# The convolution taps of the up-projection and the product behind them, each issued one step later

## Chip, core and metric

The kernel runs on one core of a Trainium2 chip. The metric is the device time of one execution in microseconds, as the median of several runs. TensorE (PE) does the matrix products, VectorE (DVE) and ScalarE (ACT) the elementwise work, GpSimd (POOL) and SyncE (SP) issue transfers here.

## What is computed

The reference is one decoder layer on 512 tokens of width 1024: three token mixers, a merge, and a gated MLP with a causal convolution of width 3. The change lies in the MLP's first half:

```
def causal_dwconv3(u, w, b):
    up = jnp.pad(u, ((0, 0), (2, 0), (0, 0)))
    return up[:, :s] * w[0] + up[:, 1:s + 1] * w[1] + up[:, 2:] * w[2] + b
...
    h2 = rmsnorm(x, g_ffn)
    a, b = jnp.split(h2 @ w_up, 2, axis=-1)
    a = causal_dwconv3(a, ffn_conv_w, ffn_conv_b)
    x = x + (jax.nn.silu(a) * b) @ w_down
```

The hidden width is 2816, which is 22 blocks of 128 channels. One block f of a with the same block of b is called a pair here.

## The kernel before

All data are float32. Since TensorE takes rounded operands, each operand is cut in two: a high half (hi, ScalarE, a rounding copy) and a low half (lo, VectorE, source minus hi), and a product is three matmuls (hi with hi, lo with hi, hi with lo). Each low half therefore waits for its high half. Weights come from memory in pieces of 128x1024 (ra, rb, raw), issued by SP.

The up-projection is laid out by hand. A list `steps` holds what TensorE does, one step after the other, and a table `jobs` holds what the other engines do behind each step. `at(i, job)` puts a job behind step i. `later(gen, 0)` runs a generator up to its first `yield` now, and every further part one step later. What lands in the table first is issued first, and VectorE, ScalarE, POOL and SP work in exactly that order in this stretch.

Pairs 6 to 20 are fast pairs: instead of eight half-size products (128x256 outputs over four blocks of depth) they use seven, with sums of weights and sums of inputs. A step is one such product, 12 matmuls. The head of a pair is four steps with the outputs y, z, x, w, the tail three steps that add to z, x, w. The order is head f, tail f-1, head f+1, tail f. Even pairs use the banks s, m, s, m, odd pairs four banks acc; two pairs later the banks are used again. The lines that matter, by engine:

- VectorE: 1199 and 1203 form the sums of weights (sx); 1222, 1223 and 1227 add up the head's outputs; 1244 forms another weight sum; 1250 and 1257 empty z and w behind the tail, 1257 into u, the padded input of the convolution; 998 is the low half of a cut; 1077 the two taps; 1094 (or 1087 for four pairs whose result is stored to memory and read back) the product of the Silu with b.
- ScalarE: 986 is the high half of a cut; 990 a negative of it, to which POOL's accumulating transfer (993) adds the source; 1218 and 1254 copy y and x out; 1074 the first tap with the bias; 1081 the Silu.
- POOL: 1200 adds one weight piece to another by an accumulating transfer (ra gets raw or rb added); the cut of ra waits for it.

In `taps_of` line 1074 is issued behind the tail's last step, the taps one step later, the Silu one more, and the product one more. `taps_of` is called for pairs 0 and 1 by `first_pairs` and for each fast pair by `p3_done`.

Of the kernel before, what the change touches and what calls it, by code (L numbers as in the profile page):

```python
# [123 lines left out]
def layer_kernel(ctx: ExitStack, tc: tile.TileContext, xT, memT, vecs, ws, outT):  # L124
# [22 lines left out]
    def tmp(n=S, dt=F32):  # L147

        i = tmps[0]
        if i is not None:  # L150
            tmps[0] = (i + 1) % 10
            if i >= 8:
                return cm.tile([P, n], dt, tag="tmp", name=nm("tmp"), bufs=2)
        return tp.tile([P, n], dt, tag="tmp", name=nm("tmp"), bufs=8)
# [743 lines left out]
    def taps(f):  # L898
        return [V("f_w", NF * i + f) for i in range(3)], V("f_b", f)
# [170 lines left out]
    def taps_of(f, u, b):  # L1070

        ws, bias = taps(f)
        t = tmp()
        nc.scalar.activation(t, u[:, 0:S], AF.Identity, bias=bias, scale=ws[0])
        yield
        for i in (1, 2):
            nc.vector.scalar_tensor_tensor(
                t, u[:, i : S + i], ws[i], t, op0=ALU.mult, op1=ALU.add
            )
        yield  # L1080
        nc.scalar.activation(t, t, AF.Silu)
        yield
        gate_up(f, b, t)

    def gate_up(f, b, t):
        if f in SPILL:
            nc.vector.tensor_mul(t, b, t)
            nc.sync.dma_start(md[f], t)
            mf[f] = None
            return  # L1090
        n = sum(m is not None for m in mf.values())
        pool, tag = (fm, "mf") if n < NF - 8 - len(SPILL) else (mp, "mj")
        m = pool.tile([P, S], F32, tag=tag, name=nm("mf"))
        nc.vector.tensor_mul(m, b, t)
        mf[f] = m
# [9 lines left out]
    def first_pairs():  # L1105
        for f in range(2):
            u, b = padded(), tmp()
            nc.vector.tensor_mul(u[:, 2 : S + 2], accs[2 * f], r2b)
            nc.vector.tensor_mul(b, accs[2 * f + 1], r2b)
            later(taps_of(f, u, b), 0)  # L1110
# [126 lines left out]
    def fast_tail(f, q):  # L1237
        t = len(steps)
        i2 = 2 * (f - 2) + 3
        n = KH * P  # L1240

        def sums_4():
            sx = q["sx"]
            nc.vector.tensor_sub(sx[:, :n], raws[base + i2][:, :n], sx[:, :n])  # L1244

        w2 = cut_raw(i2, t, t + 1, by_dma=True, lead=LEAD + 3)
        w4 = cut_at(t + 2, t + 2, lambda: q["sx"][:, :n], known=lambda h: at(h - 2, sums_4))

        def p4_done():
            nc.vector.tensor_add(q["b"][:, :H], q["z"][:, :H], q["v"][:, H:])  # L1250
            q["u"] = padded()

        def p2_done():
            nc.scalar.activation(q["u"][:, 2 : H + 2], q["x"][:, :H], AF.Copy)

        def p3_done():
            nc.vector.tensor_add(q["u"][:, H + 2 :], q["w"][:, :H], q["v"][:, H:])
            later(taps_of(f, q["u"], q["b"]), 0)

        steps.extend((  # L1260
            (lambda: product(q["z"], w2, KH, sums[3], False), p4_done),
            (lambda: product(q["x"], w2, 0, rows(KH, 0), False), p2_done),
            (lambda: product(q["w"], w4, 0, rows(KH, H), False), p3_done),
        ))
# [133 lines left out]
```

## Time and profile before

| | |
|---|---|
| median of 3 runs (lowest to highest) | 827.24 us (827.23 to 827.34) |
| profiled execution, and its span | 826.2 us, 824.4 us |
| TensorE busy | 815.3 us, 99% of the span |
| TensorE weight loads | 695.0 us, 84% |
| VectorE busy | 569.7 us, 69% |
| ScalarE busy | 436.3 us, 53% |
| POOL busy | 95.7 us, 12% |
| granted TensorE clock | 1.00 in every stretch (2.4 GHz) |

The span runs from the first to the last instruction of the profiled execution; its time also holds what lies around that. The shares are averages over stages: the fast pairs run from about 534 to 687 us, and in them VectorE is much busier than over the span as a whole.

### The profile page before, as it was taken

The page shows a single profiled execution, that of the slowest core. Times are in us where ns is not written, and L with a number is a line of the kernel's source. Part 1 is how long each engine was busy: PE and PEld are TensorE (multiplying, and loading weights), DVE is VectorE, ACT ScalarE, POOL GpSimd, SP SyncE. Part 2 cuts the span into 40 slices and gives each one's busy share as a digit, 9 for nine tenths or more (in the row PEclk, how much of TensorE's full clock was granted, in tenths as well). Part 3 has the DMA queues.
Part 4 walks back from the last instruction along what each step waited for, and adds up shares of the span by engine and source line. Part 5 has one row for each costly group of instructions (what it writes and reads, how often), then busy time and mean ns, then how long its engine had stood idle before and what let it go on. Part 6 is the DMA issues. An engine that isn't in the chain of part 4 may idle for free.

```text
span 824.4 us, 11450 instructions
## 1 busy us (share of the span) xinstructions
PE 815.3 (99%) x4254; PEld 695.0 (84%) x4254; DVE 569.7 (69%) x963; ACT 436.3 (53%) x779; POOL 95.7 (12%) x134
## 2 busy tenths in 40 slices
PE   9999999999999999999999999999999999999998
PEld 7888788888888888888888888899999998888888
DVE  6998898957767777666466587768888888523221
ACT  7676776736655645554334476556656568312210
POOL 0300000101221011110000022222222220000000
PEclk9999999999999999999999999999999999999999
DMA  8453122333332332225334375677777886433310
GB/s 304 131 179 105 58 96 77 117 120 97 118 100 90 107 97 77 80 100 179 102 99 145 126 197 150 156 182 174 180 179 179 206 191 219 140 102 130 113 64 26
DMA packets 38263, 109.08 MB, mean 132 GB/s; under 512 B 4416, under 2 KB 5056, under 8 KB 38080
## 3 DMA queue, kind: packets, MB, share of 16 engines
q1 hardware_dynamic: 29856, 93.34, 33.9%
q0 software_dynamic: 8208, 14.95, 10.6%
q8 instruction: 33, 0.54, 0.3%
q14 instruction: 22, 0.18, 0.1%
q10 hardware_dynamic: 144, 0.08, 0.0%
HBM read 85.01 MB, written 5.24 MB: 109 GB/s over the span
## 4 chain that ended last, share of the span: by engine, by line
PE 77%; DMA 8%; issue 7%; DVE 3%; POOL 3%; ACT 1%; SPq 0%; POOLq 0%; ACTq 0%; DVEq 0%
PE acc L258 19%; PE acc L259 19%; PE acc L260 19%; DMA ra<-raw 5%; PE s L259 4%; PE s L260 4%; PE s L258 4%; POOL lo L993 2%; DMA ra<-rb 2%; PE m L774 1%; PE m L1184 1%; DMA raw<-ws 1%; PE m L260 1%; PE m L259 1%; PE m L258 1%
## 5 line engine op out<-in xcount | busy, mean ns | idle before, releaser
L223 DVE TENSOR_TENSOR lo<-raw,hi 128x1024 fp32r<-128x1024 f32 (+2 forms) x106 | 128.9, 1216 | 126.4 <-ACT hi L220 125.9
L220 ACT ACTIVATE hi<-raw 128x1024 fp32r<-128x1024 f32 (+2 forms) x106 | 110.3, 1041 | 151.1 <-PE acc L260 85.3
L260 PE MATMUL acc<-h,hi 128*128 128x512 f32 x360 | 142.1, 395 | 0.0
L259 PE MATMUL acc<-h,lo 128*128 128x512 f32 x360 | 142.1, 395 | 0.0
L258 PE MATMUL acc<-h,hi 128*128 128x512 f32 x360 | 142.1, 395 | 0.0
L260 PEld LDWEIGHTS acc<-h,hi 128*128 128x128 f32 x360 | 67.7, 188 | 16.1
L259 PEld LDWEIGHTS acc<-h,lo 128*128 128x128 f32 x360 | 67.7, 188 | 15.3
L258 PEld LDWEIGHTS acc<-h,hi 128*128 128x128 f32 x360 | 67.7, 188 | 15.2
L259 PE MATMUL acc<-m,lo 128*128 128x512 f32 (+1 forms) x132 | 47.2, 358 | 0.0
L258 PE MATMUL acc<-m,hi 128*128 128x512 f32 (+1 forms) x132 | 47.2, 358 | 0.0
L260 PE MATMUL acc<-m,hi 128*128 128x512 f32 (+1 forms) x132 | 47.1, 357 | 0.0
L1184 PE MATMUL acc<-t,hi 128*128 128x256 f32 x224 | 43.5, 282 | 0.0
L1184 PE MATMUL m<-t,hi 128*128 128x256 f32 x192 | 38.7, 284 | 1.9 <-DVE tmp L1250 1.9
L986 ACT ACTIVATE hi<-sx 128x1024 fp32r<-128x1024 f32 (+1 forms) x30 | 25.2, 839 | 25.2 <-DVE sx L1244 19.7
L323 ACT ACTIVATE ty<-ty 32x16 f32<-32x16 f32 (+4 forms) x136 | 29.1, 214 | 17.2 <-DVE ty L331 8.2
L1184 PEld LDWEIGHTS acc<-t,hi 128*128 128x128 f32 x224 | 36.1, 190 | 0.0
L1184 PEld LDWEIGHTS m<-t,hi 128*128 128x128 f32 x192 | 31.4, 190 | 2.7 <-DVE tmp L1250 2.7
L720 POOL TENSOR_SCALAR_AFFINE_SELECT S<-S 128x128 f32<-128x128 f32 x32 | 13.0, 415 | 168.4 <-ACT S L718 167.8
L993 POOL DMA_DIRECT2D lo<-raw x28 | 24.5, 1028 | 67.8 <-ACT lo L990 67.8
L1184 PE MATMUL acc<-hn,hi 128*128 128x256 f32 x168 | 32.3, 282 | 0.0
L1184 PE MATMUL acc<-t,lo 128*128 128x256 f32 x112 | 31.6, 282 | 0.0
L802 ACT ACTIVATE tmp<-acc,half_b 128x512 f32<-128x512 f32 x21 | 14.5, 688 | 29.9 <-PE acc L260 29.8
(308 smaller groups left out, 2050.1 us busy)
## 6 DMA issues: line engine op xcount, KB each, us to landing
raw<-ws SPq DMA_DIRECT2D x120, 512.0 KB, 3.3
ra<-ws SPq DMA_DIRECT2D x20, 512.0 KB, 4.0
lo<-raw POOLq DMA_DIRECT2D x28, 256.0 KB, 4.3
ra<-raw POOLq DMA_DIRECT2D x11, 256.0 KB, 5.4
rb<-ws SPq DMA_DIRECT2D x5, 512.0 KB, 4.8
lo<-rb POOLq DMA_DIRECT2D x10, 256.0 KB, 4.3
xr<-xT SPq DMA_DIRECT2D x8, 256.0 KB, 5.6
xres<-xT SPq DMA_DIRECT2D x1, 2048.0 KB, 9.6
```

The costliest lines, as they stand in the source:

```text
L220: nc.scalar.activation(hi[:, :m], raw[:, :m], AF.Copy)
L223: nc.vector.tensor_sub(lo[:, :m], raw[:, :m], hi[:, :m].bitcast(F32))
L258: nc.tensor.matmul(out, l[0], r[0], start=start, stop=False)
L259: nc.tensor.matmul(out, l[1], r[0], start=False, stop=False)
L260: nc.tensor.matmul(out, l[0], r[1], start=False, stop=stop)
L323: nc.scalar.activation(dst, src, AF.Copy)
L720: nc.gpsimd.affine_select(dg, dg, pattern=[[1, P]], compare_op=ALU.is_ge, fill=NEG, base=0, channel_multiplier=-1,)
L774: nc.tensor.matmul(acc[:, i0:], l, b[:, : S - i0], start=i == 0 and b is x[0], stop=i == 3 and b is x[1],)
L802: nc.scalar.activation(z, acc, AF.Tanh, bias=half_b[:, i : i + 1], scale=0.5)
L986: nc.scalar.activation(out[0], a, AF.Copy)
L993: nc.gpsimd.dma_start(out[1][:, c], a[:, c], accum_op=ALU.add)
L1184: nc.tensor.matmul(out[:, :H], a, b, start=first and k == 0 and x == 0, stop=k == KH - 1 and x == 2, skip_group_check=not first,)
```

## The change

Two `yield` are added in `taps_of`, the function that handles the convolution, the Silu and the product of pairs 0, 1 and 6 to 20. The taps are issued two steps behind the tail's last step instead of one, the Silu three instead of two, the product five instead of three.

```
         nc.scalar.activation(t, u[:, 0:S], AF.Identity, bias=bias, scale=ws[0])
         yield
+        yield
         for i in (1, 2):
             nc.vector.scalar_tensor_tensor(
                 t, u[:, i : S + i], ws[i], t, op0=ALU.mult, op1=ALU.add
             )
         yield
         nc.scalar.activation(t, t, AF.Silu)
+        yield
         yield
         gate_up(f, b, t)
```

In the changed file lines 1077 and 1081 become 1078 and 1082, and every line behind them in this stretch is two further down (1094 becomes 1096, 1250 becomes 1252).

VectorE's rows from one write of u to the next, in the middle of the fast pairs (the pair whose u is in tile u_4528), before:

```order
L1257 TENSOR_TENSOR u_4528<-acc_5965,tmp_5966 128x256
L998 TENSOR_TENSOR lo_6200<-sx_5921,hi_6199 128x512
L1077 SCALAR_TENSOR_TENSOR tmp_6216<-u_4528,vec,tmp_6216 128x512 x2
L998 TENSOR_TENSOR lo_6220<-sx_6183,hi_6219 128x1024
L1094 TENSOR_TENSOR mf_6262<-tmp_6031,tmp_6216 128x512
L1222 TENSOR_TENSOR tmp_6228<-acc_6226,tmp_6228 128x256
L1223 TENSOR_TENSOR tmp_6228<-acc_6225,tmp_6228 128x256
L1227 TENSOR_TENSOR tmp_6293<-acc_6227,tmp_6228 128x256
L998 TENSOR_TENSOR lo_6279<-ra_6034,hi_6278 128x1024
L1244 TENSOR_TENSOR sx_6052<-raw_5905,sx_6052 128x512
L1250 TENSOR_TENSOR tmp_6162<-m_6094,tmp_6097 128x256
```

The same place on VectorE in the changed kernel:

```order
L1259 TENSOR_TENSOR u_4528<-acc_5963,tmp_5964 128x256
L998 TENSOR_TENSOR lo_6200<-sx_5921,hi_6199 128x512
L998 TENSOR_TENSOR lo_6220<-sx_6183,hi_6219 128x1024
L1078 SCALAR_TENSOR_TENSOR tmp_6216<-u_4528,vec,tmp_6216 128x512 x2
L1224 TENSOR_TENSOR tmp_6226<-acc_6224,tmp_6226 128x256
L1225 TENSOR_TENSOR tmp_6226<-acc_6223,tmp_6226 128x256
L1229 TENSOR_TENSOR tmp_6291<-acc_6225,tmp_6226 128x256
L998 TENSOR_TENSOR lo_6277<-ra_6032,hi_6276 128x1024
L1246 TENSOR_TENSOR sx_6052<-raw_5903,sx_6052 128x512
L1096 TENSOR_TENSOR mf_6299<-tmp_6029,tmp_6216 128x512
L1252 TENSOR_TENSOR tmp_6160<-m_6092,tmp_6095 128x256
```

The taps stand behind the 128x1024 low half of sx, and the product stands behind three sums, the low half of ra and line 1246 (1244 before).

ScalarE's rows of the same pair, in the changed kernel:

```order
L1074 ACTIVATE tmp_6216<-u_4528,vec 128x512
L986 ACTIVATE hi_6219<-sx_6183 128x1024
L1220 ACTIVATE tmp_6226<-acc_6222 128x256
L986 ACTIVATE hi_6241<-raw_5903 128x1024
L990 ACTIVATE lo_6242<-raw_5903 128x1024
L1082 ACTIVATE tmp_6216<-tmp_6216 128x512
L986 ACTIVATE hi_6276<-ra_6032 128x1024
```

They stand in the same order as before: no other job of ScalarE lies in the steps that the Silu is moved past. TensorE's order is the same throughout. On SP the four stores of line 1088 stand behind two weight loads that they stood ahead of.

## Rows read from the trace of the kernel before

**Rows 1.** Waits of TensorE (engine line, waited for, us total, times, longest us).

```profile
PE m L1184 <- DVE tmp L1250: 1.9, 4, 1.0
```

**Rows 2.** VectorE in order of time, one pair: start, length, instruction, [idle before, releaser].

```profile
622.53 0.42 DVE L1257 TENSOR_TENSOR u<-acc,tmp 128x256 f32<-128x256 f32 x1
...
623.89 1.54 DVE L1077 SCALAR_TENSOR_TENSOR tmp<-u,vec,tmp 128x512 f32<-128x512 f32 x2 [0.35 <-ACT tmp L1074]
625.34 1.22 DVE L998 TENSOR_TENSOR lo<-sx,hi 128x1024 fp32r<-128x1024 f32 x1
627.52 0.69 DVE L1094 TENSOR_TENSOR mf<-tmp,tmp 128x512 f32<-128x512 f32 x1 [0.96 <-ACT tmp L1081]
628.13 0.42 DVE L1222 TENSOR_TENSOR tmp<-acc,tmp 128x256 f32<-128x256 f32 x1
...
629.45 1.22 DVE L998 TENSOR_TENSOR lo<-ra,hi 128x1024 fp32r<-128x1024 f32 x1
630.58 0.69 DVE L1244 TENSOR_TENSOR sx<-raw,sx 128x512 f32<-128x512 f32 x1
631.18 0.42 DVE L1250 TENSOR_TENSOR tmp<-m,tmp 128x256 f32<-128x256 f32 x1
...
632.24 0.69 DVE L1203 TENSOR_TENSOR sx<-raw,sx 128x512 f32<-128x512 f32 x1
632.85 0.42 DVE L1257 TENSOR_TENSOR u<-m,tmp 128x256 f32<-128x256 f32 x1
```

**Rows 3.** ScalarE in order of time, the same pair.

```profile
623.04 0.82 ACT L1074 ACTIVATE tmp<-u,vec 128x512 f32<-128x512 f32 x1 [1.42 <-DVE u L1257]
623.76 1.04 ACT L986 ACTIVATE hi<-sx 128x1024 fp32r<-128x1024 f32 x1
...
625.92 1.04 ACT L990 ACTIVATE lo<-raw 128x1024 fp32r<-128x1024 f32 x1
626.87 0.62 ACT L1081 ACTIVATE tmp<-tmp 128x512 f32<-128x512 f32 x1
627.39 1.04 ACT L986 ACTIVATE hi<-ra 128x1024 fp32r<-128x1024 f32 x1
```

**Rows 4.** TensorE in order of time: tail's z of pairs 8, 12, head's z of 16.

```profile
564.76 0.28 PE L1184 MATMUL m<-t,hi 128*128 128x256 f32 x1
...
604.84 0.28 PE L1184 MATMUL m<-t,hi 128*128 128x256 f32 x1
...
631.66 0.39 PE L1184 MATMUL m<-t,hi 128*128 128x256 f32 x1 [0.36 <-DVE tmp L1250]
```

**Rows 5.** VectorE's line 1250 of pairs 6 and 18, TensorE's z of 20.

```profile
548.10 0.42 DVE L1250 TENSOR_TENSOR tmp<-m,tmp 128x256 f32<-128x256 f32 x1
...
673.04 0.42 DVE L1250 TENSOR_TENSOR tmp<-m,tmp 128x256 f32<-128x256 f32 x1
...
673.52 0.38 PE L1184 MATMUL m<-t,hi 128*128 128x256 f32 x1 [0.29 <-DVE tmp L1250]
```

**Rows 6.** A Silu that waits for its taps, in order of time, VectorE and ScalarE.

```profile
675.03 1.53 DVE L1077 SCALAR_TENSOR_TENSOR tmp<-u,vec,tmp 128x512 f32<-128x512 f32 x2
...
676.60 0.63 ACT L1081 ACTIVATE tmp<-tmp 128x512 f32<-128x512 f32 x1 [1.64 <-DVE tmp L1077]
```

**Rows 7.** The accumulating transfer's issue on POOL, and cuts of ra behind it.

```profile
559.72 0.86 POOL L1200 DMA_DIRECT2D ra<-rb  x1 [3.49 <-DVE sx L1199]
...
566.45 1.06 ACT L986 ACTIVATE hi<-ra 128x1024 fp32r<-128x1024 f32 x1 [1.42 <-PE m L1184]
...
567.55 1.22 DVE L998 TENSOR_TENSOR lo<-ra,hi 128x1024 fp32r<-128x1024 f32 x1 [0.47 <-ACT hi L986]
...
622.18 0.86 POOL L1200 DMA_DIRECT2D ra<-raw  x1 [3.49 <-DVE sx L1199]
...
649.60 1.06 ACT L986 ACTIVATE hi<-ra 128x1024 fp32r<-128x1024 f32 x1 [1.48 <-PE s L1184]
```

**Rows 8.** VectorE in order of time, ahead of the first fast pair's tail.

```profile
537.83 0.42 DVE L1222 TENSOR_TENSOR tmp<-s,tmp 128x256 f32<-128x256 f32 x1 [1.30 <-PE s L1184]
```

More of the change, by code (lines that the diff above doesn't have):

```diff
@@ L1075, in taps_of @@
         yield
+        yield
         for i in (1, 2):
@@ L1081, in taps_of @@
         nc.scalar.activation(t, t, AF.Silu)
+        yield
         yield
```

## The prediction

> **What bounds the kernel now.** Read the busy shares first: TensorE is busy 99% of the span, so nothing here can gain much, and a change to VectorE's order counts only where TensorE comes to wait for VectorE. The next view is what TensorE waits for: over the whole span, the largest entry is line 1184 (a product of a fast pair, bank m) waiting for VectorE's line 1250, four times, 1.9 us together [rows 1]. This lies in the stretch that the diff touches.
>
> The third view is the order of time there. One fast pair on VectorE runs from line 1257 at 622.53 to the next at 632.85, 10.32 us [rows 2]. TensorE without waiting goes from 564.76 to 604.84 in four pairs, 10.02 us each [rows 4]. So VectorE is slower than TensorE by 0.3 us per pair although it idles twice in each: 0.35 us before the taps (for ScalarE's line 1074) and 0.96 us before the product (for the Silu) [rows 2]. ScalarE is what it waits for: line 1074 starts 0.51 us after line 1257, then come the cut of sx, the copy, the cut of raw and its negative, and only then, without a pause, the Silu at 626.87 [rows 3]. The two engines form a loop: u, ScalarE's row of work, product, the rest of VectorE's row, next u.
>
> What this costs TensorE: the z product of an even pair waits until line 1250 of two pairs earlier has emptied the bank; 1250 starts at 631.18 and the product at 631.66, 0.48 us later [rows 2, 4]. Line 1250 of pair 6 is at 548.10, that of pair 18 at 673.04, and TensorE's product at 673.52 again follows by 0.48 [rows 5]. So twelve pairs took 124.94 us on VectorE, and TensorE's z product of pair 20 is released by it. At 10.02 per pair it would have been there earlier: the tail's z of pair 12 starts at 604.84, the head's z of pair 14 four products later (4/7 of 10.02, 610.57), that of pair 20 six pairs on, 670.69. The loss today is 2.8 us.
>
> **The change part by part.** On VectorE the taps (line 1077, two instructions) pass one row, the low half of the cut of sx (128x1024); the product passes five, lines 1222, 1223, 1227, the low half of ra and line 1244. In the fast stretch nothing moves on ScalarE: 1074, cut of sx, copy, cut of raw, its negative, Silu, cut of ra. That decides it.
>
> What goes: both gaps of VectorE in their old places, 0.35 + 0.96 us. The product now comes where the Silu is long done.
>
> What comes instead: right behind line 1257 VectorE now wants the low half of sx, whose high half ScalarE cuts only after line 1074, which itself waits for 1257. And since the taps are later, the Silu is, and the cut of ra behind it on ScalarE, and VectorE's low half of ra waits for that. The new loop, from start to start: 1257 to 1074, 0.51 (622.53 to 623.04); 1074 to the cut of sx, 0.72 [rows 2, 3]; a high half to the low half that waits for it, 1.10 (566.45 to 567.55) [rows 7]; low half to the next on VectorE, 1.13 (629.45 to 630.58) [rows 2]; taps to a Silu that waits for them, 1.57 (675.03 to 676.60) [rows 6]; Silu to the cut of ra, 0.52 [rows 3]; high to low half of ra, 1.10; low half to line 1244, 1.13; 1244 to the product, 0.60 (as 1244 to 1250 now); product to 1250, 0.61 (as product to 1222 now); 1250 to 1203, 1.06; 1203 to 1257, 0.61 [rows 2]. Sum: 10.66 us, against 10.32 now. The other path to the Silu, through the negative of raw (it ends 4.4 us after line 1257) [rows 2, 3], is shorter than that through the taps (5.0 us), so the taps set it.
>
> For scale, the handovers on VectorE: the next row starts 0.07 to 0.09 us before the one ahead of it ends (629.45 plus 1.22 against 630.58) [rows 2]. The Trainium skill (VectorE: DVE Perf Modes, The DRAIN you can't avoid) says that the next operation doesn't start until the pipe is empty, with an exception for instructions that aren't held; by full durations the six handovers of the loop would add about 0.5 us a pair, and the sum below would be 6 us larger. The rows decide for start to start.
>
> Twelve rounds from line 1250 of pair 6 (no row ahead of it in this stretch moves) to that of pair 18: 12 x 10.66 = 127.92, against 124.94, which is **3.0 us** later. The 124.94 hold what late transfers cost now; the new loop pays for them separately: the cut of ra waits for an accumulating transfer that POOL issues 0.35 us before line 1257 (622.18) [rows 2, 7]. In the new loop the cut is reached 5.55 + 0.35 = 5.9 us after that issue. A pair where the transfer lands later pays all of it: 559.72 to 566.45 is 6.73, 0.83 too late, and the one at 649.60, with 1.48 us of idle instead of 1.42, is alike [rows 7]. (The rows name TensorE as releaser; both wait for several things, and I take the transfer to be the last.) Two such pairs make 1.7 us. Low end none, high end 1.7; the accumulation starts 0.6 us later behind the weight loads than now, since the product stands between, which may shorten or move the overlap: I take half, **0.8 us**.
>
> From the z product of pair 20 on, TensorE's work is the same and VectorE lags by the same share, so the delay is carried to the end. Smaller edits, at nothing: in the first pairs two products move behind the taps of pair 2, covered by VectorE's wait for TensorE before the first fast pair (1.30 us at 537.83) [rows 8], at worst 1.2 us for two products without that cover; the stores of four spilled tiles go behind two weight loads on SP, which then don't wait for the product any more; the last pairs' products fall into a stretch where VectorE prepares inputs that TensorE wants much later.
>
> Sum against the profiled execution: span 824.4 + 3.8 = 828.2, its time 826.2 + 3.8 = 830.0. The median of the runs is 827.24, 1.0 above that execution, so **831.0 us**.
>
> **The rivals.**
> *Faster: the gaps are simply gone.* If the high half of sx is ready whenever VectorE comes to it, VectorE needs 10.32 - 1.31 = 9.0 us a pair [rows 2], less than TensorE's 10.02, and TensorE's whole loss goes: 827.24 - 2.8 = 824.4. It decides from the point where the new loop is under 10.02, 0.64 less than my sum. For it: both gaps sit exactly at the two moved places. The Trainium skill (Perfetto Trace Analysis, Optimization Strategy) gives this reading too: find the gaps of the contended engine and let what they wait for be done sooner. Against it: ScalarE's order keeps the cut of sx behind line 1074.
> *No change one can measure* (a measurement of this kernel can tell about 0.2%, 1.65 us): the loop is at most (124.94 + 1.65)/12 = 10.55, 0.11 shorter than my sum, because one or two handovers taken from other places are shorter here, and no landing is late. At 10.5 it is 126.0 - 124.94 = 1.1 us, 828.3.
> *Much slower: landings.* With the cut of ra on the loop, every late landing counts. If half of the twelve pairs pay 0.85 us it is 3.0 + 5.1 = 8.1, 835.3. Against it: only two of the pairs show so long a wait now.
>
> **How the numbers follow.** Forecast (3.0 to 4.7 later, 830.2 to 831.9) 0.72; much slower 0.10; no change 0.11; faster 0.07. Slower by over 0.2% is 0.72 + 0.10 = 0.82. An error of 0.05 us in the loop is 0.6 us in the time; with that on both ends, and the no-change case taken in below and part of the landings above, the range is 828.3 to 833.5, which leaves out the faster case and the worst landings.
>
> **What would show it.** In the changed trace: VectorE's idle before the low half of sx of 1.2 to 1.4 us and before the low half of ra of 0.4 to 0.5 us in each fast pair, none before taps and product; line 1257 to 1257 at 10.6 to 10.8 us; ScalarE idle before the Silu, waiting for the taps; TensorE's waits for line 1250 (two lines further down) about 4 to 7 us in total, at the z product of even pairs from pair 10 or 12 on. Wrong if the low half of sx doesn't wait, or if TensorE waits less than now.

## The result, and the profile after

The changed kernel took 831.14 us (median of 5 runs, 830.34 to 831.97) against 827.33 us for the kernel before on the same chip (5 runs, 827.23 to 827.48). The ratio is 1.0056, 95% interval 1.0044 to 1.0069: 3.8 us slower. The profiled execution took 831.14 us, its span is 829.3 us, 4.9 us more than the span before. One run of the kernel before, at 1624.92 us nearly twice as long as the 15 others of its set, is left out of the comparisons below.

The page of the changed kernel (first part: busy time, share of the span, instructions):

```profile
span 829.3 us, 11475 instructions
...
PE 814.3 (98%) x4254; PEld 693.8 (84%) x4254; DVE 570.0 (69%) x963; ACT 436.6 (53%) x779; POOL 95.8 (12%) x134
```

The work is the same on every engine, to within 1.2 us. What grew is waiting. The waits of TensorE in the changed kernel (engine line, waited for, us total, times, longest us):

```profile
PE m L1186 <- DVE tmp L1252: 5.7, 5, 1.7
...
PE s L259 <- DVE lo L223: 1.2, 1, 1.2
```

The first row answers to [rows 1]: 5.7 us instead of 1.9. The second lies in the first 35 us of the program, far ahead of the change (0.5 us in the kernel before); over the first 100 us waits of that kind make everything behind them 0.5 us later in this execution than in the one of before.

One pair on VectorE in order of time, changed kernel (start, length, instruction, [idle before, releaser]), to lay beside [rows 2]:

```profile
614.89 0.42 DVE L1259 TENSOR_TENSOR u<-m,tmp 128x256 f32<-128x256 f32 x1
615.22 0.68 DVE L998 TENSOR_TENSOR lo<-sx,hi 128x512 fp32r<-128x512 f32 x1
617.20 1.23 DVE L998 TENSOR_TENSOR lo<-sx,hi 128x1024 fp32r<-128x1024 f32 x1 [1.30 <-ACT hi L986]
618.35 1.54 DVE L1078 SCALAR_TENSOR_TENSOR tmp<-u,vec,tmp 128x512 f32<-128x512 f32 x2
...
621.53 1.22 DVE L998 TENSOR_TENSOR lo<-ra,hi 128x1024 fp32r<-128x1024 f32 x1 [0.33 <-ACT hi L986]
622.67 0.69 DVE L1246 TENSOR_TENSOR sx<-rb,sx 128x512 f32<-128x512 f32 x1
623.27 0.68 DVE L1096 TENSOR_TENSOR mf<-tmp,tmp 128x512 f32<-128x512 f32 x1
623.87 0.42 DVE L1252 TENSOR_TENSOR tmp<-acc,tmp 128x256 f32<-128x256 f32 x1
...
625.54 0.42 DVE L1259 TENSOR_TENSOR u<-acc,tmp 128x256 f32<-128x256 f32 x1
```

And ScalarE, the same pair, beside [rows 3]:

```profile
615.40 0.82 ACT L1074 ACTIVATE tmp<-u,vec 128x512 f32<-128x512 f32 x1 [2.03 <-DVE u L1259]
616.13 1.04 ACT L986 ACTIVATE hi<-sx 128x1024 fp32r<-128x1024 f32 x1
...
618.29 1.04 ACT L990 ACTIVATE lo<-rb 128x1024 fp32r<-128x1024 f32 x1
619.91 0.63 ACT L1082 ACTIVATE tmp<-tmp 128x512 f32<-128x512 f32 x1 [0.58 <-DVE tmp L1078]
620.45 1.04 ACT L986 ACTIVATE hi<-ra 128x1024 fp32r<-128x1024 f32 x1
```

Both old gaps are gone: the taps (line 1078) and the product (line 1096) wait for nothing. In their place VectorE waits 1.30 us before the low half of sx and 0.33 us before the low half of ra, and ScalarE waits 0.58 us before the Silu (line 1082) for the taps. Line 1259 to 1259 takes 10.65 us, against 10.32 for line 1257 before. The moved waits are longer together (1.63 us) than the two they replace (1.31 us).

VectorE's line 1252 of pairs 6 and 18, and TensorE's z product of pair 20 that the second one releases, beside [rows 5]:

```profile
548.61 0.42 DVE L1252 TENSOR_TENSOR tmp<-m,tmp 128x256 f32<-128x256 f32 x1
...
677.83 0.42 DVE L1252 TENSOR_TENSOR tmp<-m,tmp 128x256 f32<-128x256 f32 x1
...
678.30 0.39 PE L1186 MATMUL m<-t,hi 128*128 128x256 f32 x1 [0.97 <-DVE tmp L1252]
```

Twelve pairs took 677.83 - 548.61 = 129.22 us, against 124.94 before: 4.3 us later. Ten of the twelve take 10.64 to 10.71 us, the other two 11.33 and 11.38; the kernel before has the same two long pairs (10.88 and 10.94 among ten at 10.29 to 10.32). So about 4.0 us are the longer ordinary pair, twelve times 0.33, and only 0.2 us are the long pairs. With the 0.5 us from the program's start (548.61 against 548.10) that is 4.8 of the span's 4.9 us.

### The profile page after: what moved, and what is told of

It is laid out like the page before. It is cut to its first block, busy times and chain, and to the rows that moved or that the text cites. A ratio compares the mean times of both kernels' runs of the same rounds, so it can differ in the third digit from the quotient of the medians.

```text
span 829.3 us, 11475 instructions
## 1 busy us (share of the span) xinstructions
PE 814.3 (98%) x4254; PEld 693.8 (84%) x4254; DVE 570.0 (69%) x963; ACT 436.6 (53%) x779; POOL 95.8 (12%) x134
## 4 chain that ended last, share of the span: by engine, by line
PE 75%; DVE 10%; DMA 5%; ACT 5%; issue 5%; POOL 1%; SPq 0%; DVEq 0%; ACTq 0%; POOLq 0%
PE acc L258 19%; PE acc L259 19%; PE acc L260 19%; PE s L259 4%; PE s L260 4%; PE s L258 4%; ACT hi L986 3%; DMA ra<-rb 2%; DMA raw<-ws 2%; DVE lo L998 1%; DVE tmp L1078 1%; PE m L774 1%; DMA ra<-raw 1%; DVE sx L1246 1%; PE m L260 1%
## 5 line engine op out<-in xcount | busy, mean ns | idle before, releaser
L998 DVE TENSOR_TENSOR lo<-sx,hi 128x1024 fp32r<-128x1024 f32 (+1 forms) x30 | 28.6, 954 | 16.9 <-ACT hi L986 16.9
```

Source lines behind the costliest of these rows:

```text
L998: nc.vector.tensor_sub(out[1], src(), out[0].bitcast(F32))
```

## The experiments

Two theories stand against each other. **The loop**: VectorE and ScalarE wait for each other in a ring, 1259 to 1074 to the cut of sx to VectorE's low half to the taps to the Silu to the cut of ra to VectorE's low half to 1246, product, 1252, 1259, and only what lies on that ring counts. **The rival**: the later position of the taps or of the product is bad in itself (a later Silu, a later product), so that each half of the change costs its share. What the prediction held as its own rival, that the gaps go and nothing comes for them, is tried by the same kernels.

The first four kernels ran on one chip, where the kernel before had a median of 826.08 us (29 runs). The last three ran together in a second set, with the kernel before at 826.26 us (15 runs). Each ratio is the one on record; it need not be the quotient of the two medians (0.9982 for the first kernel, where 0.9974 is on record).

### Only the taps one step later

```
         nc.scalar.activation(t, u[:, 0:S], AF.Identity, bias=bias, scale=ws[0])
         yield
+        yield
         for i in (1, 2):
```

> Only the first yield of the change: taps, Silu and product each one step later, so that the taps stand behind the low half of sx and the product between the second and the third sum of the head, ahead of the low half of ra. Theory (the loop over both engines, in which each row has its place): the loop up to the low half of ra is that of the changed kernel, 6.65 us behind the write of u, but the product now lies in VectorE's wait for the cut of ra instead of behind it, so 0.6 us leaves the loop: 10.05 us a pair, level with TensorE's 10.02; TensorE hardly waits, and the time is about 824.5 us, 2.8 below the kernel before. Rival (later taps by themselves cost, because the Silu and the cut of ra come late): as slow as the changed kernel, about 831.

Measured: 824.59 us (12 runs, 823.03 to 826.65), ratio to before 0.9974 (0.9960 to 0.9988). VectorE in order of time, one pair, and TensorE's wait for the line that empties z (1251 in this file):

```profile
622.12 1.23 DVE L998 TENSOR_TENSOR lo<-sx,hi 128x1024 fp32r<-128x1024 f32 x1 [1.29 <-ACT hi L986]
...
625.50 0.68 DVE L1095 TENSOR_TENSOR mf<-tmp,tmp 128x512 f32<-128x512 f32 x1
...
626.44 1.23 DVE L998 TENSOR_TENSOR lo<-ra,hi 128x1024 fp32r<-128x1024 f32 x1
...
629.85 0.42 DVE L1258 TENSOR_TENSOR u<-m,tmp 128x256 f32<-128x256 f32 x1
```

```profile
PE m L1185 <- DVE tmp L1251: 0.3, 1, 0.3
```

The wait of 1.29 us before the low half of sx is there in full, so the taps alone bring it. But the product (line 1095) still stands ahead of the low half of ra, and fills the time in which ScalarE makes the Silu and cuts ra: that low half waits for nothing in the pair shown, and in nine of the twelve. Line 1258 goes from 619.81 to 629.85, 10.04 us, where 10.05 was expected, and TensorE's matmuls wait 0.3 us in all. So the first half of the change alone is a gain of 1.5 us by the medians.

### Only the product one step later

```
         nc.scalar.activation(t, t, AF.Silu)
         yield
+        yield
         gate_up(f, b, t)
```

> Only the second yield: taps and Silu where they were in the kernel before, the product one step later, between the second and the third sum of the head. Theory: VectorE keeps its 0.35 us wait before the taps, the 0.96 us wait before the product goes and nothing comes in its place, because the cut of ra on ScalarE doesn't hang on the taps (it follows the negative of raw and the Silu, 4.9 us behind the write of u; the low half of ra 6.0 us behind it). Loop about 9.4 us, under TensorE's 10.02: TensorE waits for nothing in this stretch, about 824.5 us. Rival (the product ahead of line 1250 or 1252 costs by itself): slower than the kernel before.

Measured: 824.18 us (12 runs, 822.79 to 825.59), ratio 0.9969 (0.9956 to 0.9983). VectorE in order of time and TensorE's wait:

```profile
620.71 1.54 DVE L1077 SCALAR_TENSOR_TENSOR tmp<-u,vec,tmp 128x512 f32<-128x512 f32 x2 [0.35 <-ACT tmp L1074]
...
624.34 0.69 DVE L1095 TENSOR_TENSOR mf<-tmp,tmp 128x512 f32<-128x512 f32 x1
...
625.29 1.23 DVE L998 TENSOR_TENSOR lo<-ra,hi 128x1024 fp32r<-128x1024 f32 x1
...
629.10 0.43 DVE L1258 TENSOR_TENSOR u<-m,tmp 128x256 f32<-128x256 f32 x1 [0.33 <-PE m L1185]
```

```profile
PE m L1185 <- DVE tmp L1251: 0.4, 1, 0.4
```

The taps keep their old wait of 0.35 us for line 1074; the product's 0.96 us [rows 2] is gone, and in this pair nothing took its place, because the Silu keeps its old time and the cut of ra too. A pair without a new wait takes 9.35 us (line 1251 from 588.28 to 597.63), about the 9.4 expected. In eight of the twelve pairs VectorE, now early, waits 0.47 to 2.69 us before the low half of ra instead, for a cut that comes late; little of that reaches TensorE, whose matmuls wait for line 1251 once, 0.4 us. Line 1258 once waits for TensorE (0.33 us at 629.10). Each half alone is a gain, the two together a loss: no share of the loss belongs to either half, which is against the rival.

### The whole change, with line 1074 one step later as well

```
         ws, bias = taps(f)
+        yield
         t = tmp()
         nc.scalar.activation(t, u[:, 0:S], AF.Identity, bias=bias, scale=ws[0])
         yield
         for i in (1, 2):
...
         nc.scalar.activation(t, t, AF.Silu)
         yield
+        yield
         gate_up(f, b, t)
```

VectorE's order is that of the changed kernel. On ScalarE the cut of sx comes ahead of line 1074 (1075 here).

> The changed kernel with line 1074 one step later too, which puts ScalarE's cut of sx ahead of it; VectorE's order is that of the changed kernel. Theory: VectorE's low half of sx no longer waits 1.3 us, since its high half hangs on the weight sum and not on u; taps 2.3, Silu 3.9 to 4.0, low half of ra 5.6, next write of u 9.6 us behind the last one. Under 10.02: about 824.5 us with both moves of the change in place. Rival (later taps or the later product cost whatever ScalarE's order is): about 831.

Measured: 824.16 us (12 runs, 822.59 to 826.62), ratio 0.9970 (0.9956 to 0.9984). ScalarE, then VectorE, in order of time:

```profile
620.65 1.06 ACT L986 ACTIVATE hi<-sx 128x1024 fp32r<-128x1024 f32 x1 [1.63 <-DVE sx L1205]
621.62 0.80 ACT L1075 ACTIVATE tmp<-u,vec 128x512 f32<-128x512 f32 x1
```

```profile
620.54 0.42 DVE L1259 TENSOR_TENSOR u<-acc,tmp 128x256 f32<-128x256 f32 x1
...
621.75 1.22 DVE L998 TENSOR_TENSOR lo<-sx,hi 128x1024 fp32r<-128x1024 f32 x1 [0.20 <-ACT hi L986]
...
626.08 1.23 DVE L998 TENSOR_TENSOR lo<-ra,hi 128x1024 fp32r<-128x1024 f32 x1 [0.34 <-ACT hi L986]
...
630.09 0.42 DVE L1259 TENSOR_TENSOR u<-m,tmp 128x256 f32<-128x256 f32 x1
```

The high half of sx no longer waits for line 1074, which waits for line 1259. VectorE's wait ahead of its low half falls from 1.30 to 0.20 us, and the pair takes 9.55 us (620.54 to 630.09) where 9.6 was expected. Three of the twelve pairs are that short; the others take up to 10.74 us, since the low half of ra waits longer in them (up to 1.54 us). TensorE has no wait for line 1252 left. With VectorE's order unchanged, and that of POOL and SP too, ScalarE's order alone decides between 3.8 us slower and 1.9 us faster. So the stores' later place on SP, which this kernel shares, is not what the changed kernel loses by.

### The whole change, with one more operation of ScalarE on the ring

```
         nc.scalar.activation(t, t, AF.Silu)
+        nc.scalar.activation(t, t, AF.Copy)
         yield
         yield
         gate_up(f, b, t)
```

> The changed kernel with one more ScalarE row right behind the Silu: a copy of the 128x512 tile onto itself (about 0.53 us to the next row), which changes no value. Theory: the Silu and the cut of ra behind it lie on the loop, so each pair is 0.53 us longer, 12 x 0.53 = 6.4 us, less about 1.1 since the late transfers then land in time: about 836.4 us, loop 11.2 us. Rival (ScalarE, busy 6.4 of 10.7 us a pair, has room and the row is hidden): about 831, no change against the changed kernel.

Measured: 838.67 us (4 runs, 836.07 to 839.09), ratio 1.0132 (1.0107 to 1.0157). ScalarE in order of time, and TensorE's wait:

```profile
621.75 0.63 ACT L1082 ACTIVATE tmp<-tmp 128x512 f32<-128x512 f32 x1 [0.58 <-DVE tmp L1078]
622.41 0.63 ACT L1083 ACTIVATE tmp<-tmp 128x512 f32<-128x512 f32 x1
622.95 1.04 ACT L986 ACTIVATE hi<-ra 128x1024 fp32r<-128x1024 f32 x1
```

```profile
PE m L1187 <- DVE tmp L1253: 8.5, 6, 2.2
```

The ring took it up in full, and more than was expected: 11.30 us per pair (558.54, 569.85, 581.16 for line 1253), 0.65 more than without the copy. A copy of the Silu's own result starts 0.66 us behind it (621.75 to 622.41); I had priced it at the 0.53 us that ScalarE takes from one independent operation of this size to the next. That the difference comes from reading the result just written is likely, but no run separates it. All twelve pairs take 11.30 or 11.31 us, so the late transfers no longer show, as expected: twelve pairs from 547.24 to 682.89 are 135.65 us, 6.4 and 7.3 us more than in the two profiles of the changed kernel (129.22, and 128.36 in the next run). The medians differ by 8.3 us (from the 830.36 us of the next run, on another chip), the ratios by 0.74%, which is 6.1 us. The rival, 831 us, is out.

### The changed kernel again, beside the next two

> The changed kernel as it is, beside the experiments on their chip. The loop theory: +3.8 us against the kernel before there, as on the first chip (826.1 + 3.8 = 829.9 us); loop of 10.65 us in the trace. Against it: with both gaps of VectorE merely moved, a second chip would show no difference (826.1).

Measured: 830.36 us (5 runs, 830.02 to 833.30), ratio 1.0058 (1.0041 to 1.0075). In its trace line 1259 to 1259 is 10.64 us (585.25 to 595.88), and twelve pairs from line 1252 at 551.67 to 680.03 take 128.36 us, 0.86 less than in the first profile of the same kernel. The difference is the late transfers: here they add 0.7 us to twelve times 10.64, there 1.4 us.

### The first sum and the accumulating transfer one step earlier

In the changed kernel's `sums_at`:

```
-            at(h - 2, sums_1)
+            at(h - 3, sums_1)
             at(h - 1, sums_2)
```

> The changed kernel with the first sum of sx and the accumulating transfer behind it one step earlier, ahead of the product. If the two long pairs (11.3 us instead of 10.65) come from the transfer that lands late, both disappear, and ScalarE's cut of ra waits for no transfer. The loop is 10.54 us (line 1246 to 1201 0.60, to the product 0.60, to 1252 0.61, to 1205 0.34, to 1259 0.61, instead of 0.60 + 0.60 + 1.06 + 0.61 from 1246 to 1259), 1.3 us less in twelve pairs; the landings give 1.4 us, and 1252 stands 0.6 us later in its pair: 2.1 us below the changed kernel, 827.8 us beside 829.9. If the long pairs have another cause they stay, and it is 0.7 us, 829.2.

Measured: 830.70 us (5 runs, 829.05 to 830.83), ratio to before 1.0048 (1.0034 to 1.0061): no gain that can be told from 830.36. The expectation failed. The accumulating transfer's issue on POOL and ScalarE's cut of ra behind it, first in the changed kernel, then here:

```profile
560.63 0.86 POOL L1202 DMA_DIRECT2D ra<-rb  x1 [3.88 <-DVE sx L1201]
```

```profile
567.22 1.06 ACT L986 ACTIVATE hi<-ra 128x1024 fp32r<-128x1024 f32 x1 [0.58 <-DMA ra<-rb]
```

```profile
559.89 0.86 POOL L1202 DMA_DIRECT2D ra<-rb  x1 [2.88 <-PE acc L1186]
```

```profile
567.72 1.06 ACT L986 ACTIVATE hi<-ra 128x1024 fp32r<-128x1024 f32 x1 [1.01 <-DMA ra<-rb]
```

The ring is shorter as expected (line 1259 from 572.69 to 583.21, 10.52 us), but the transfer, issued 0.74 us earlier, landed 0.5 us later (line 1259 of that pair stands at nearly the same time in both, 560.98 and 561.05), and both long pairs stayed: 11.6 us, 1.1 more than the others, where it had been 0.7. Twelve pairs from 549.60 to 677.38 take 127.78 us, 0.6 less than in the run above, and the first of these times stands about 0.6 us later in its pair: nothing is left. The wait is one for the transfer, as the releaser shows, but in this run the earlier issue did not make it land earlier. The stretch of the changed kernel's trace from 564.40 to 566.80, just ahead of the landing (us; busy time and instructions of PE, PEld, DVE, ACT and POOL; granted clock, DMA share, GB/s):

```profile
564.40:566.80 2.40, 2.40 (x23) 2.40 (x22) 2.29 (x5) 1.65 (x3) 1.09 (x2) 1.00 0.10 26
```

The mean busy share of the 16 DMA engines is a tenth, at 26 GB/s: as much as one or two of them carry, so the transfer's end seems to hang on one or two while the others stand idle (this view does not name them). Why it ends late, and in which pairs, no run here tells. In the first profile of the changed kernel and in this run it was two pairs whose accumulation has rb as its source, while a third with that source was in time; in the second profile a pair with raw as its source was the latest (0.38 us of wait at 676.59). It stays open.

### Only the product later, with the same extra operation of ScalarE

```
         nc.scalar.activation(t, t, AF.Silu)
+        nc.scalar.activation(t, t, AF.Copy)
+        yield
         yield
         gate_up(f, b, t)
```

> Only the product one step later, as in the run of that alone, with the same in-place copy of the Silu's result on ScalarE that cost 0.65 us per pair in the changed kernel. In this order the low half of ra is reached on VectorE 5.95 us behind u, just when ScalarE's cut of it comes ready; the copy moves that cut 0.66 us back. The loop with the copy is 0.52 + 0.72 + 0.95 + 0.26 + 0.95 + 0.94 on ScalarE to the Silu, 0.66 to the copy, 0.54 to the cut of ra, 1.10 to the low half, 1.13 + 0.60 + 0.33 + 0.72 + 0.61 on VectorE to the next u: 10.03 us, TensorE's own pace. The loop theory: at most 1 us above the run without the copy, 824.2 to 825.2 us, VectorE waiting about 0.65 us before the low half of ra. The rival, that a further instruction of ScalarE costs its time in each pair whatever the order: 12 x 0.65 = 7.8 us, 832.

Measured: 824.65 us (11 runs, 823.20 to 826.45), ratio 0.9978 (0.9967 to 0.9989), beside 824.18 without the copy in the other set. ScalarE's Silu, copy and cut of ra, VectorE's product and low half, and TensorE's wait:

```profile
626.02 0.62 ACT L1081 ACTIVATE tmp<-tmp 128x512 f32<-128x512 f32 x1
626.67 0.63 ACT L1082 ACTIVATE tmp<-tmp 128x512 f32<-128x512 f32 x1
627.21 1.05 ACT L986 ACTIVATE hi<-ra 128x1024 fp32r<-128x1024 f32 x1
```

```profile
627.33 0.69 DVE L1096 TENSOR_TENSOR mf<-tmp,tmp 128x512 f32<-128x512 f32 x1 [0.82 <-ACT tmp L1082]
...
628.28 1.23 DVE L998 TENSOR_TENSOR lo<-ra,hi 128x1024 fp32r<-128x1024 f32 x1
```

```profile
PE m L1186 <- DVE tmp L1252: 0.4, 1, 0.4
```

The copy that cost the changed kernel 6 to 8 us costs 0.5 us by the medians here, of two sets on two chips. VectorE waits 0.82 us for it ahead of the product, not ahead of the low half of ra as I had written, since the copy holds back both and the product comes first in the row. The pair from 1252 at 620.02 to the next at 630.03 is 10.01 us, as the sum said (10.03), and that is TensorE's own pace; the way through the product happens to be as long as the one through the low half that I had summed. Five of the twelve pairs are longer, one of them 11.69 us, where the low half of ra waits for a late cut. TensorE's matmuls wait 0.4 us in all by this view.

TensorE's own rows tell the kernels apart more finely than the medians. From the head's z product of pair 8 to that of pair 20 it needs 12 x 10.02 = 120.24 us if it waits for nothing. It took 123.03 us before (550.49 to 673.52), 127.27 and 126.61 in the two profiles of the changed kernel (551.03 to 678.30, 553.89 to 680.50), 126.64 with the earlier sum, 120.64 with the taps alone, 120.79 with the product alone, 120.25 with line 1074 moved as well, 133.47 with the copy on the ring, and 121.71 with the product and the copy. By these rows the copy costs 6.2 to 6.9 us in the changed kernel's order and 0.9 us in the other. An operation costs what it adds to the ring, and that only from the point where the ring is longer than 10.02 us. Even then a little is covered: before, twelve pairs on VectorE took 4.7 us more than TensorE's 120.24 and TensorE lost only 2.8, so VectorE starts with a lead of about 1.9 us (an estimate from these rows).

## Why the prediction was right, step by step

**The loop.** Forecast 10.66 us from twelve handovers, measured 10.65 (614.89 to 625.54). Each step holds to 0.03 us: 1259 to 1074 0.51, to the cut of sx 0.73, to the low half 1.07 (taken 1.10), to the taps 1.15 (1.13), to the Silu 1.56 (1.57), to the cut of ra 0.54 (0.52), to the low half 1.08 (1.10), to 1246 1.14 (1.13), to the product 0.60, to 1252 0.60 (0.61), to 1259 1.67 (1.06 + 0.61). The start-to-start intervals of the kernel before carried over to another order of the same instructions. The Trainium skill (VectorE: DVE Perf Modes, The DRAIN you can't avoid) says that the next operation doesn't start until the pipe is empty, and that one which is not held starts earlier. Here the trace agrees with the second part: the low half of ra at 621.53 is 1.22 us long, and the next row starts at 622.67, 0.08 us before its end. With full durations the sum was about 0.5 us a pair larger, 11.2, and the trace decides for 10.65.

**Twelve rounds.** Forecast 127.92, 3.0 later than before. Measured 12 x 10.65 = 127.8 without the late transfers, 2.9 later. The 124.94 that this is held against contain 1.2 us of late landings (the two long pairs before); ring against ring it is 4.0 us.

**The late landings.** Taken at 0.8 us, with 0 and 1.7 as ends. Measured 1.4 us in the first profile (0.68 and 0.73, in the two pairs that the prediction had named), 0.7 in the second of the same kernel. Half of the 1.7 was too little in the first. Of the 1.4 us, 1.2 were paid before too, inside the 124.94. The reading that [rows 7] hide a transfer behind the releaser PE is borne out: for the same two pairs of the changed kernel the trace names the transfer itself. What doesn't hold is the working of that term, 5.9 us from the issue to the cut and all of a longer landing added, as if a landing were a fixed time behind its issue: the run with the earlier issue refutes it.

**The sum.** 3.0 + 0.8 forecast; in the profile 2.9 + 1.4 on the pairs and 0.5 from the start of the program, which the change has nothing to do with, 4.9 with rounding. The medians differ by 3.8 us, as forecast. That the total fits to 0.1 us is chance in part: the landings were 0.6 us larger than taken and the program's start 0.5 us later, 1.1 us that the sum lacked; and I added 1.0 us to get from the profiled execution to the median, while the profiled execution of the changed kernel lies at its median. The two errors cancel. The mechanism and the size of the ring did not need that luck.

**Smaller edits at nothing.** Right so far as it shows: from TensorE's z of pair 20 to the end of the span it was 150.9 us before [rows 5] and is 151.0 now.

**What would show it.** VectorE's idle of 1.2 to 1.4 us before the low half of sx: 1.30. Of 0.4 to 0.5 before that of ra: 0.33, a little less. ScalarE waiting for the taps before the Silu: 0.58. TensorE waiting 4 to 7 us in all at z of even pairs from pair 10 or 12 on: 5.7 us, five times, from pair 12 on.

**The rivals.** *The gaps are simply gone* (824.4): it fails on the step that was held against it, that ScalarE's cut of sx stands behind line 1074. With that one line moved, the same order of VectorE gives 824.16; with either half of the change alone, 824.59 and 824.18, on a chip where the kernel before has 826.08. That is 1.5 to 1.9 us by the medians, less than the 2.8 us that I took for the whole loss; the three intervals reach to 3.3 us and more, so they don't exclude it, and by TensorE's rows above the gains are 2.4, 2.2 and 2.8 us: with line 1074 moved as well the whole loss is gone. The Trainium skill (Perfetto Trace Analysis, Optimization Strategy) says to find the gaps of the contended engine and make what they wait for start sooner. The runs agree where what is waited for does come no later, and in the changed kernel it came later, because moving the taps moved the Silu and the cut behind it. *No change*: the loop would have had to be 10.55. *Much slower*: two pairs of twelve paid, not six.

## What to carry to other kernels

A gap on an engine that stands in a ring with another is not free time: before moving an instruction out of a gap, add up the ring in the new order, start to start, from the rows of the old trace, with everything that the other engine holds in its own order, and compare the sum with the pace of the engine that bounds the kernel. Here the same instructions gave 10.65, 10.32, 10.04, 9.55 and 9.35 us in a pair without a late transfer, depending on two or three positions, and only what was above 10.02 cost anything. Two moves that each gain can lose together: the product that moved away was what filled the wait that the moved taps opened.

## What the runs showed of the hardware beyond that

TensorE's granted clock can fall behind a pause of its own, and not every time. In the run with the copy on the ring, TensorE stood 2.20 us and went on at 615.55; the stretches before and after, and one behind an earlier pause (columns: us, PE busy and matmuls, granted clock, DMA share, GB/s):

```profile
609.60:613.20 3.60, 3.60 (x32) 1.00 0.47 79
616.40:619.70 3.30, 3.30 (x18) 0.50 0.96 282
592.90:596.50 3.60, 3.56 (x30) 1.00 1.00 318
```

From 616.4 to 619.7 the clock was 0.50, which is 1.2 GHz, and 18 matmuls were started in 3.3 us instead of 32 in 3.6. The third stretch lies behind a pause of 2.22 us that ended at 592.94, and there it stayed at 1.00. Behind a third pause, of 2.19 us to 660.76, it was 0.50 again until 664.0. VectorE sets the pace there, so TensorE's next wait was shorter for each fall, 0.84 us (638.16) and 0.80 us (683.36) instead of 2.2. In the second profile of the changed kernel the same fall came behind a wait of 1.17 us that ended at 35.70, with the clock at 0.50 until 39.0. The same wait in the first profile ended at 34.38 and was followed by none; there the three waits of 0.25 us just ahead of it are missing. In the first 40 us no later wait makes it up: that execution had line 1252 of pair 6 at 551.67 instead of 548.61, of which 1.3 us were there ahead of the fall (35.70 against 34.38) and about 1.7 us are the fall (an estimate: half of 3.3 us), and took 833.30 us, the longest of its five.
